# Softmax division moved behind the product with the values, the reciprocals broadcast through DRAM

## The chip, the cores and the metric

The kernel runs on one core of a Trainium2 chip. A core has five engines that run side by side, each with its own queue in program order: TensorE (PE, matrix products into PSUM), VectorE (DVE), ScalarE (ACT), GpSimd (POOL) and SyncE (SP, which here only issues DMAs). ACT and POOL issue DMAs too. The metric is the device time of one execution in microseconds (us); lower is better.

## The reference

Two layers of an encoder over 1024 tokens of width 1024. Layer 0 mixes tokens by windowed attention (16 query heads of 64, four key/value heads, a window of 128 to each side, a learned sink per head in the softmax); layer 1 by a gated linear recurrence (HGRN2). Each mixer also carries four cross-attention heads of 128 into 256 memory tokens. After each mixer comes a convolutional feed-forward part. What the change touches are the two softmaxes:

```python
# window attention (layer 0)
m = jnp.maximum(jnp.max(s, axis=-1, keepdims=True), sk)
p = jnp.exp(s - m)
p = p / (jnp.sum(p, axis=-1, keepdims=True) + jnp.exp(sk - m))
o = jnp.einsum('bnhgqk,bnkhd->bnqhgd', p.astype(v.dtype), vb)

# cross-attention into the memory (both layers)
p = jax.nn.softmax(s, axis=-1)
o = jnp.einsum('bhtm,bmhd->bthd', p.astype(v.dtype), v)
```

The sum belongs to a query and is the same for all values, so dividing the probabilities before the product or the result after it gives the same output up to rounding.

## The kernel before

All arithmetic is float32. Each operand of a matrix product is split into a high part (rounded to the matrix format, float32r) and a low part (the rest), and a product is two or three matmuls (`mm3`, lines 80 to 83). The split is a cast on ACT and a subtraction on DVE (`split`, lines 85 to 87), so nearly every product needs both of them first.

The program runs in stages: `start` (memory keys and values, transposed input), `window` (layer 0's mixer), the output projection `wo0`, `ffn` of layer 0, `hgrn` (layer 1's mixer), `wo1`, `ffn` of layer 1. The instructions are written down in program order, but the order on each engine is made by a planner that simulates a timeline with estimated costs (line 1559) and takes, among the instructions that are ready, those written earlier first; `tc.high_priority` and `tc.issue_after` bend this at single places. Within an engine's queue the resulting order is fixed: an instruction that waits holds up all behind it. Tiles come from pools with a number of buffers per tag; a tile whose buffers are all in use makes its writer wait until the oldest is free.

**Window attention** (`window`, lines 243 to 430). For each of the four key/value groups g, `proj(g)` computes queries, keys and values of its four heads, and `attend(g)` works in blocks of 128 queries, 32 blocks in all. A block, for its four heads j, makes the scores on PE (`ps`, two banks, L363 and L364), adds the mask and takes the maximum on DVE (L366), exponentiates on ACT with the sum as a by-product (L373), adds the sink and takes the reciprocal `rd`, 128 x 4, queries over partitions (L378, L379). It then multiplies the probabilities `sm` by `rd`: heads 0 and 1 on ACT (L382), 2 and 3 on DVE (L384). For each of two or three key tiles PE transposes the probabilities into `pt` (L389), they are split into `ph` and `pl`, and PE multiplies with the values into `po` (one bank, L392 and L393). The values stand in `v` as 64 columns of high part and 64 of low part, so that `po` holds on partitions 0 to 63 and 64 to 127 two halves of the output, transposed: value dimension over partitions, four heads times 128 queries along the free axis. ACT copies the upper half out (L395) and DVE adds the lower half (L396) into `o`, a tile of 64 partitions that takes a pair of blocks (two buffers). SP stores each pair to the DRAM tensor `oT` (L407), or for the last group into `ul` directly (L401), from where `split_moved` splits it.

**Cross-attention** (`cross_unit`, lines 198 to 240) handles one of four heads h and one half b of the tokens (512) in a unit. Eight units run inside `attend` of layer 0 (two each in the first two groups, four in the third), eight in layer 1's `hgrn`, in its heads 0 to 3. A unit projects its queries, makes scores for four query tiles, takes maximum, exponential, sum and reciprocal (L217 to L226), multiplies the probabilities `xp` by the reciprocals on DVE (L228, four instructions of 128 x 256), transposes (L233), splits, and multiplies with the values into `po`. ACT copies the result to `xo` (L239; one buffer; in layer 1 its tag is `ot`, shared with the recurrence's outputs, and the last unit uses the tile of the probabilities) and issues its store to `oT` itself (L240). In layer 0 the bank `po` is the one that the window blocks use; in layer 1 the two halves use different banks.

On SP's queue in these stages stand the weight loads (`wunit`, L75: DMA into the staging tile `st`, cast on ACT, subtraction on DVE or for some units on GpSimd, L77), the memory keys and values (L192), the stores of `o`, and the output projection's reads of `oT` (L456, L472). On GpSimd stand the additions of the rotary embedding (L288, L289) and DMAs that sum weights for the feed-forward part (L142, L144).

Of the kernel before, what the change touches and what calls it, by code (L numbers as in the profile page):

```python
# [8 lines left out]
F32 = mybir.dt.float32  # L9
# [3 lines left out]
AF = mybir.ActivationFunctionType  # L13
ALU = mybir.AluOpType
# [4 lines left out]
P = 128  # L19
# [28 lines left out]
def build(tc, A, out):  # L48
    nc = tc.nc
    act, dve, pool, pe = nc.scalar, nc.vector, nc.gpsimd, nc.tensor  # L50
    bc = lambda ap, shape: ap.to_broadcast(shape)

    dram = tc.alloc_tile_pool(name="dram", bufs=1, space=DRAM)
    oT = [dram.tile([12, P, T], F32, name=f"oT{l}") for l in range(2)]
# [95 lines left out]
        next(x)  # L150

    kvd = [dram.tile([4, P, 2, 256], F32, name=f"kvd{l}") for l in range(2)]

    def memory_kv(tp, psb, mh, ml, first, rsb, rsm, step):
        held = []
# [42 lines left out]
    def cross_unit(l, h, b, head, wp, tags, w0, pair, dead=False):  # L198

        wh, wl, kvh, kvl = head  # L200
        ps = tags["pj"][2].tile([P, 512], F32, tag=tags["pj"][0], bufs=tags["pj"][1], name="pj")
        for k in range(KT):
            c = slice(k * P, (k + 1) * P)
            m = slice(b * 512, (b + 1) * 512)
            mm3(ps, wh[:, c], wl[:, c], uh[:, k, m], ul[:, k, m], k == 0, k == KT - 1)
        xh, xl = pair("x", b)
        with tc.high_priority(AHEAD):
            split(xh, xl, ps)
        p = wp.tile([P, 4, 256], F32, tag="sm", bufs=tags["sm"], name="xp")
        st = {x: wp.tile([P, 4], F32, tag=x, name=x) for x in ("nm", "su", "rd")}  # L210
        for i in range(2):
            s = tags["ps"][2].tile([P, 2, 256], F32, tag=tags["ps"][0], bufs=tags["ps"][1], name="ps")
            for j in range(2):
                m = slice((2 * i + j) * P, (2 * i + j + 1) * P)
                mm3(s[:, j, :], xh[:, m], xl[:, m], kvh[:, 0, :], kvl[:, 0, :], True, True)
            e = slice(2 * i, 2 * i + 2)
            dve.reduce_max(st["nm"][:, e], s, axis=AX.X)  # L217
            if l == 0:
                dve.tensor_tensor(st["nm"][:, e], st["nm"][:, e], xsc[:, 1, 4 * b + 2 * i:4 * b + 2 * i + 2], op=ALU.mult)
            else:  # L220
                dve.tensor_scalar_mul(st["nm"][:, e], st["nm"][:, e], -XSCALE)
            for j in range(2):
                q = 2 * i + j
                act.activation(p[:, q, :], s[:, j, :], AF.Exp, bias=st["nm"][:, q:q + 1],
                               scale=xsc[:, 0, 4 * b + q:4 * b + q + 1] if l == 0 else XSCALE, accum_out=st["su"][:, q:q + 1])
        dve.reciprocal(st["rd"], st["su"])  # L226
        for q in range(4):
            dve.tensor_scalar_mul(p[:, q, :], p[:, q, :], st["rd"][:, q:q + 1])  # L228
        po = tags["po"][b]()
        for m in range(2):  # L230
            tp = tags["pt"][2].tile([P, 4, P], F32, tag=tags["pt"][0], bufs=tags["pt"][1], name="pt")
            for q in range(4):
                pe.transpose(tp[:, q, :], p[:, q, m * P:(m + 1) * P], ident)  # L233
            ph, pl = pair("p", m)
            split(ph, pl, tp.rearrange("p a b -> p (a b)"))
            hd = slice(m * P, (m + 1) * P)
            mm3(po, kvh[:, 1, hd], kvl[:, 1, hd], ph, pl, m == 0, m == 1)
        ot = p[:, :2, :].rearrange("p a b -> p (a b)") if dead else w0.tile([P, 512], F32, tag=tags.get("xo", "xo"), bufs=1, name="xo")
        act.copy(ot, po)  # L239
        act.dma_start(oT[l][8 + h, :, b * 512:(b + 1) * 512], ot)  # L240


    def window():
# [4 lines left out]
        wmask = ap_.tile([P, 384], F32, bufs=1, name="wmask")  # L248
        sk = ap_.tile([P, 16], F32, bufs=1, name="sk")
        sk8 = ap_.tile([P, 16], F32, bufs=1, name="sk8")  # L250
        ap_.tile([64, 4, 256], F32, tag="o", bufs=2, name="o")
        nc.sync.dma_start(wmask, A["wmask"])
        nc.sync.dma_start(sk, A["a_sink"].to_broadcast([P, 16]))
        c4 = lambda ap: ap.rearrange("p (h a c) -> p h a c", a=2, c=32)
# [80 lines left out]
        pairs, roped = {}, {}  # L335
# [9 lines left out]
        def attend(g, qkv, blocks=range(NT)):  # L345
            qs, kh, kl, v = qkv
            for b in range(2):
                for nn in range(4):
# [1 line left out]
                    if n not in blocks:  # L350
                        continue
                    if nn % 2 == 0:
                        pairs[0] = ap_.tile([64, 4, 256], F32, tag="o", bufs=2, name="o")
                    o = pairs[0]
                    lo, hi = max(n - 1, 0), min(n + 2, NT)
                    w = (hi - lo) * P
                    mo = (lo - (n - 1)) * P
# [19 lines left out]
                            split_moved()  # L377
                    dve.tensor_tensor(st["su"], st["su"], st["es"], op=ALU.add)  # L378
                    dve.reciprocal(st["rd"], st["su"])  # L379
                    for j in range(4):  # L380
                        if j < 2:
                            act.activation(sm[:, j, :w], sm[:, j, :w], AF.Copy, scale=st["rd"][:, j:j + 1])  # L382
                        else:
                            dve.tensor_scalar_mul(sm[:, j, :w], sm[:, j, :w], st["rd"][:, j:j + 1])  # L384
                    po = psp.tile([P, 4, P], F32, tag="po", bufs=1, name="po")
                    for c in range(hi - lo):
                        tp = psp.tile([P, 4, P], F32, tag="pt", bufs=2, name="pt")
# [4 lines left out]
                        pe.matmul(po, v[:, lo + c, :], ph, start=c == 0, stop=False)  # L392
                        pe.matmul(po, v[:, lo + c, :], pl, start=False, stop=c == hi - lo - 1)  # L393
                    ov = o[:, :, (nn % 2) * P:(nn % 2 + 1) * P]
                    act.copy(ov, po[64:])  # L395
                    dve.tensor_tensor(ov, po[:64], ov, op=ALU.add)  # L396
                    if nn % 2 == 1 and g == 3:
                        ts_ = slice((n - 1) * P, (n + 1) * P)
                        moved.append(ts_)
# [1163 lines left out]
```

## Time and profile before

| | |
|---|---|
| median of 3 runs | 2662.74 us (2661.32 to 2666.62) |
| profiled execution, first to last instruction | 2663.0 us |
| TensorE busy | 2605.1 us, 98% of the span |
| VectorE, ScalarE, GpSimd busy | 1820.8, 1377.3, 468.3 us |
| mean granted TensorE clock | 0.998 |
| mean DMA rate | 160 GB/s |

The profile is one execution with the time of every instruction. A group line gives source line, engine, operation, output and input tiles, the count, the busy time and the mean of one in ns, then the time that the engine sat idle just before these instructions and what ended it. A wait line tells which engine waited at which line for which other, with the total in us, the number of times and the longest. A timeline line begins with the start and the duration in us. The view by stretches gives for each stretch (us from the span's start) the busy time and the number of instructions of each engine. Matmuls overlap, so that the busy times of single ones add up to more than the time TensorE spends.

### The profile page before, as it was taken

Reading aid. Unit: us, or ns where it says so; the run is one execution under the profiler, and the core shown is the slowest. Engines: PE = TensorE matmul, PEld = TensorE weight load, DVE = VectorE, ACT = ScalarE, POOL = GpSimd, SP = SyncE. Lnnn points to the kernel's source line nnn. Section 1 sums busy time; section 2 is a strip of 40 time slices with the busy share of each in tenths; the row PEclk is TensorE's granted clock in tenths of the full one; section 3 lists DMA queues with packets and bytes.
Section 4 is the critical chain, followed back from the end, with each engine's and each line's share of the span. In section 5 each row is a group of like instructions: output and inputs, shape, how many; then the busy total and the mean of one; then the engine's idle time right before and its main releaser. Section 6 shows DMA issues by size and latency. Waiting matters only on the chain. (4 is left out here: it accounts for less than half of the span.)

```text
span 2663.0 us, 39112 instructions
## 1 busy us (share of the span) xinstructions
PE 2605.1 (98%) x14420; PEld 2186.3 (82%) x14420; DVE 1820.8 (68%) x3043; ACT 1377.3 (52%) x2503; POOL 468.3 (18%) x520
## 2 busy tenths in 40 slices
PE   8999999999999999999999999999999999999998
PEld 7888887788888887887888888888887788888887
DVE  6778886578655565478688686887757755656447
ACT  6467676545444444455455554555534444444453
POOL 0321010211111100031224131231311111110013
PEclk9999999999999999999999999999999999999999
DMA  9772222367787857574235351103437778785666
GB/s 354 248 169 58 74 89 82 104 188 196 197 203 192 209 153 250 190 246 160 85 110 147 83 127 55 52 25 101 139 103 198 191 194 209 197 204 167 220 194 233
DMA packets 195728, 425.93 MB, mean 160 GB/s; under 512 B 20048, under 2 KB 56272, under 8 KB 189904
## 3 DMA queue, kind: packets, MB, share of 16 engines
q1 hardware_dynamic: 161552, 324.06, 37.6%
q0 software_dynamic: 24544, 90.19, 16.3%
q10 hardware_dynamic: 9440, 9.19, 1.1%
q8 instruction: 113, 1.85, 0.3%
q14 instruction: 79, 0.65, 0.1%
HBM read 330.04 MB, written 116.39 MB: 168 GB/s over the span
## 5 line engine op out<-in xcount | busy, mean ns | idle before, releaser
L87 DVE TENSOR_TENSOR wl<-st,wh 128x1024 fp32r<-128x1024 f32 (+1 forms) x238 | 263.4, 1113 | 318.4 <-ACT wh L86 308.1
L86 ACT CAST wh<-st 128x1024 fp32r<-128x1024 f32 (+1 forms) x238 | 222.5, 937 | 289.7 <-PE X L575 187.8
L81 PE MATMUL pj<-uh,wh 128*128 128x512 f32 x512 | 202.9, 397 | 4.0 <-DVE q L1118 2.0
L575 PE MATMUL X<-wl,wh 128*128 128x512 f32 x528 | 205.4, 391 | 0.3 <-DVE wl L87 0.3
L575 PE MATMUL X<-wh,wl 128*128 128x512 f32 x528 | 205.0, 390 | 0.0
L575 PE MATMUL X<-wh 128*128 128x512 f32 x528 | 199.6, 391 | 2.6 <-ACT c L989 2.1
L82 PE MATMUL pj<-ul,wh 128*128 128x512 f32 x512 | 201.7, 394 | 0.1
L83 PE MATMUL pj<-uh,wl 128*128 128x512 f32 x512 | 201.8, 394 | 0.0
L81 PE MATMUL pj<-wh,uh 128*128 128x384 f32 (+1 forms) x512 | 190.3, 373 | 4.7 <-DVE gs L1104 2.5
L83 PE MATMUL pj<-wh,ul 128*128 128x384 f32 (+1 forms) x512 | 187.7, 367 | 0.0
L82 PE MATMUL pj<-wl,uh 128*128 128x384 f32 (+1 forms) x512 | 187.3, 366 | 0.1
L77 DVE TENSOR_TENSOR wl<-st,wh 128x1024 fp32r<-128x1024 f32 (+1 forms) x91 | 116.3, 1283 | 26.0 <-ACT wh L76 25.3
L575 PE MATMUL V<-uh,wh 128*128 128x512 f32 x336 | 130.7, 389 | 0.0
L575 PE MATMUL V<-ul,wh 128*128 128x512 f32 x336 | 130.7, 389 | 0.0
L575 PE MATMUL V<-uh,wl 128*128 128x512 f32 x336 | 130.7, 389 | 0.0
L76 ACT CAST wh<-st 128x1024 fp32r<-128x1024 f32 (+1 forms) x97 | 97.7, 1013 | 44.9 <-PE pj L82 25.2
L575 PEld LDWEIGHTS X<-wh 128*128 128x128 f32 x528 | 99.5, 188 | 24.1 <-ACT c L989 2.5
L575 PEld LDWEIGHTS X<-wl,wh 128*128 128x128 f32 x528 | 99.6, 189 | 21.3 <-DVE wl L87 0.7
L575 PEld LDWEIGHTS X<-wh,wl 128*128 128x128 f32 x528 | 99.5, 188 | 20.7
L81 PEld LDWEIGHTS pj<-uh,wh 128*128 128x128 f32 x512 | 96.3, 188 | 24.2 <-DVE q L1118 3.1
L83 PEld LDWEIGHTS pj<-uh,wl 128*128 128x128 f32 x512 | 96.2, 188 | 18.6
L82 PEld LDWEIGHTS pj<-ul,wh 128*128 128x128 f32 x512 | 96.3, 188 | 18.6 <-DVE ul L87 0.4
(413 smaller groups left out, 7167.9 us busy)
## 6 DMA issues: line engine op xcount, KB each, us to landing
st<-hid SPq DMA_DIRECT2D x154, 256.0 KB, 3.0
st<-in_ffw_dram SPq DMA_DIRECT2D x108, 256.0 KB, 3.4
w2s<-in_ffw_dram POOLq DMA_DIRECT2D x24, 1024.0 KB, 8.4
st<-in_ffw_dram SPq DMA_DIRECT2D x46, 512.0 KB, 4.3
hid<-tt SPq DMA_DIRECT2D x88, 256.0 KB, 4.7
st<-w2s SPq DMA_DIRECT2D x88, 256.0 KB, 3.4
sx<-in_ffw_dram SPq DMA_DIRECT2D x84, 256.0 KB, 4.0
sy<-in_ffw_dram SPq DMA_DIRECT2D x42, 512.0 KB, 6.6
```

What stands on the lines that cost most here:

```text
L76: act.copy(h[:, :n], raw)
L77: (eng or dve).tensor_tensor(l[:, :n], raw, h[:, :n].bitcast(F32), op=ALU.subtract)
L81: pe.matmul(o, ah, bh, start=first, stop=False)
L82: pe.matmul(o, ah, bl, start=False, stop=False)
L83: return pe.matmul(o, al, bh, start=False, stop=last)
L86: act.copy(h, src)
L87: dve.tensor_tensor(l, src, h.bitcast(F32), op=ALU.subtract)
L575: last = pe.matmul(o, x, y, start=new, stop=e, skip_group_check=not first)
```

## The change

A helper `spread(dst, rd)` writes the 128 x 4 reciprocals into one of 48 rows of a new DRAM tensor `rdd`, transposed so that the four heads (or query tiles) with their 128 queries lie one behind the other, and then reads that row back into `dst`, the same row for every partition. Both DMAs are issued by SP.

In the cross-attention the four multiplications of the probabilities go. The output tile first receives the spread reciprocals, and DVE multiplies `po` by them into the same tile, in place of ACT's copy. SP issues the store, no longer ACT. In layer 1's last unit, where the output tile is that of the probabilities, the spread comes after the last transpose.

In the window attention the four multiplications (L382, L384) go. The tile `o` has 128 partitions now; the lower 64 take the result as before, in the upper 64 one half of the columns takes the unnormalised sums of the two parts of `po` (ACT's copy and DVE's addition, as before but to these partitions) and the other half the spread reciprocals; which half is which alternates with the block. GpSimd multiplies the two into the lower 64 partitions.

```diff
+    rdd = dram.tile([48, 4, P], F32, name="rdd")
+    slots = iter(range(48))
+
+    def spread(dst, rd):
+
+        row = rdd[next(slots)]
+        nc.sync.dma_start(row.rearrange("j p -> p j"), rd)
+        nc.sync.dma_start(dst, row.unsqueeze(0).to_broadcast(list(dst.shape)))
...
         dve.reciprocal(st["rd"], st["su"])
-        for q in range(4):
-            dve.tensor_scalar_mul(p[:, q, :], p[:, q, :], st["rd"][:, q:q + 1])
+        if not dead:
+            ot = w0.tile([P, 512], F32, tag=tags.get("xo", "xo"), bufs=1, name="xo")
+            spread(ot.rearrange("p (q c) -> p q c", q=4), st["rd"])
         po = tags["po"][b]()
...
-        ot = p[:, :2, :].rearrange("p a b -> p (a b)") if dead else w0.tile([P, 512], F32, tag=tags.get("xo", "xo"), bufs=1, name="xo")
-        act.copy(ot, po)
-        act.dma_start(oT[l][8 + h, :, b * 512:(b + 1) * 512], ot)
+        if dead:
+            ot = p[:, :2, :].rearrange("p a b -> p (a b)")
+            spread(ot.rearrange("p (q c) -> p q c", q=4), st["rd"])
+        dve.tensor_tensor(ot, po, ot, op=ALU.mult)
+        nc.sync.dma_start(oT[l][8 + h, :, b * 512:(b + 1) * 512], ot)
...
-                        pairs[0] = ap_.tile([64, 4, 256], F32, tag="o", bufs=2, name="o")
-                    o = pairs[0]
+                        pairs[0] = ap_.tile([P, 4, 256], F32, tag="o", bufs=2, name="o")
+                    o = pairs[0][:64]
+                    sums, rows = [pairs[0][64:, :, x * P:(x + 1) * P] for x in (nn % 2, 1 - nn % 2)]
...
                     dve.reciprocal(st["rd"], st["su"])
-                    for j in range(4):
-                        if j < 2:
-                            act.activation(sm[:, j, :w], sm[:, j, :w], AF.Copy, scale=st["rd"][:, j:j + 1])
-                        else:
-                            dve.tensor_scalar_mul(sm[:, j, :w], sm[:, j, :w], st["rd"][:, j:j + 1])
+                    spread(rows, st["rd"])
                     po = psp.tile([P, 4, P], F32, tag="po", bufs=1, name="po")
...
-                    act.copy(ov, po[64:])
-                    dve.tensor_tensor(ov, po[:64], ov, op=ALU.add)
+                    act.copy(sums, po[:64])
+                    dve.tensor_tensor(sums, po[64:], sums, op=ALU.add)
+                    pool.tensor_tensor(ov, sums, rows, op=ALU.mult)
```

2 lines of the change are left out of this document (1 added, 1 removed).

## The prediction

> **What bounds the kernel now.** I read the page's first part, then the busy time by stretch, then who kept TensorE waiting.
>
> ```profile
> PE 2605.1 (98%) x14420; PEld 2186.3 (82%) x14420; DVE 1820.8 (68%) x3043; ACT 1377.3 (52%) x2503; POOL 468.3 (18%) x520
> ```
>
> ```profile
> core 0: us, PE busy (x) PEld busy (x) DVE busy (x) ACT busy (x) POOL busy (x), PEclk, DMA share, GB/s
> 100.00:200.00 100.00, 93.17 (x519) 83.09 (x520) 74.86 (x201) 63.28 (x165) 23.07 (x31) 0.97 0.73 173
> 200.00:300.00 100.00, 96.83 (x563) 86.91 (x562) 84.14 (x224) 70.07 (x177) 14.69 (x20) 1.00 0.29 71
> 300.00:400.00 100.00, 92.58 (x533) 81.00 (x533) 81.00 (x212) 72.61 (x180) 11.26 (x16) 1.00 0.26 78
> 400.00:500.00 100.00, 95.07 (x464) 76.68 (x463) 65.84 (x166) 64.43 (x150) 0.00 (x0) 1.00 0.23 68
> 1300.00:1900.00 600.00, 592.41 (x4737) 501.38 (x4736) 464.44 (x917) 316.98 (x688) 158.24 (x166) 1.00 0.32 88
> ```
>
> TensorE computes for 98% of the span, and the edit takes no matmul and no transpose away. So it can only win TensorE's idle time, in the two stretches where attention runs: 22.4 us in 100 to 500 (the window attention of layer 0 with its eight cross-attention units), 7.6 us in 1300 to 1900 (the eight units of layer 1). Their sum, 30 us or 1.1%, is the ceiling. Who ended those waits in 100 to 500 (engine and line, total us, times, longest):
>
> ```profile
> PE ps L363 <- DVE mx L366: 8.8, 14, 1.5
> PE po L393 <- DVE pl L87: 3.4, 6, 1.2
> PE pj L81 <- DVE xl L87: 1.5, 3, 0.9
> PE po L392 <- ACT ph L86: 1.2, 2, 0.8
> PE pt L389 <- ACT sm L382: 0.8, 2, 0.6
> ```
>
> None is over 1.5 us: TensorE waits for VectorE or ScalarE because those run behind, not for one long chain. Only the last row, 0.8 us, waits for the division itself.
>
> **The change part by part.** *Removed.* Groups of instructions in 95 to 505 (busy us, mean ns of one, then the idle time before):
>
> ```profile
> L382 ACT ACTIVATE sm<-sm,rd 128x384 f32<-128x384 f32 (+1 forms) x64 | 34.1, 584 | 5.9 <-DVE rd L379 5.8
> L384 DVE TENSOR_SCALAR sm<-sm,rd 128x384 f32<-128x384 f32 (+1 forms) x64 | 23.9, 416 | 0.5
> L228 DVE TENSOR_SCALAR xp<-xp,rd 128x256 f32<-128x256 f32 x32 | 14.6, 519 | 0.4
> L239 ACT COPY xo<-po 128x512 f32<-128x512 f32 x8 | 4.6, 581 | 5.9 <-PE po L83 5.9
> L396 DVE TENSOR_TENSOR o<-po,o 64x512 f32<-64x512 f32 x32 | 21.7, 677 | 6.0 <-ACT o L395 5.9
> ```
>
> ScalarE loses 34.1 + 4.6 = 38.7 us. VectorE loses 23.9 + 14.6 and gains eight products of 128 x 512 out of PSUM in place of the copy; the nearest row is L396, 0.68 us each, so 5.4: net 33.1. (The copy and add of the two halves, L395 and L396, stay; they only write to partitions 64 to 127.) Over these 400 us VectorE's load falls from 305.8 to 272.7 (76% to 68%), ScalarE's from 270.4 to 231.7 (68% to 58%).
>
> What TensorE gets of it I estimate by how a queue's backlog shrinks, taking it as busy over idle: VectorE 0.765/0.235 = 3.26 before, 0.682/0.318 = 2.14 after, a third less. The waits of the kind above that end on a busy VectorE or ScalarE (8.8 + 3.4 + 1.5 + 1.2 + some 2.1 in smaller rows) are 17.0 us: a third is 5.8, and the 0.8 of L382 goes whole. Bounds: 0, if the order in which the planner puts the instructions passes nothing on, and 17.8.
>
> *Added on GpSimd*: 32 products of 64 x 512, both inputs in SBUF. A row for 64 partitions is missing; the nearest is the 128 x 512 product:
>
> ```profile
> L539 POOL TENSOR_TENSOR v<-v,g x4: 1294/1295/1761, 1920.7 to 1936.3; 128x512 f32<-128x512 f32 x4
> ```
>
> (min/median/max ns.) 32 x 1.295 = 41.4 us, 10% of the 400, on an engine that is at most 23% busy there. GpSimd isn't free for VectorE, though. A timeline shows it, first GpSimd's line, then VectorE's:
>
> ```profile
> 92.18 3.62 POOL L77 TENSOR_TENSOR wl<-st,wh 128x768 fp32r<-128x768 f32 x2
> ```
>
> ```profile
> 91.89 3.94 DVE L369 TENSOR_SCALAR nm<-mx 128x4 f32<-128x4 f32 x1
> ```
>
> A VectorE instruction on 4 elements a partition, else 0.16 us, lasted 3.94 us and ended at 95.83, just behind the two GpSimd products (95.80). The Trainium skill ("SBUF — State Buffer", section on the two separate sides) calls this an exclusive lock: a GpSimd instruction shuts out VectorE instructions with two SBUF inputs or in a two-port mode for its whole length. By that rule all 41.4 us could fall on VectorE and the gain would be below nothing; the row agrees on the mechanism, and how many meet is the question. In my own count, the instructions of this kind in the 400 us are nm, es and su of each block (3 x 32) and about 40 subtractions from SBUF, 136 in all; each meets a GpSimd product with 10% chance and loses half of it, 0.65 us: 8.8 us (bounds 0 and 41.4). That leaves 33.1 - 8.8 = 24.3 us of relief, load 70.4%, backlog 2.38, and the gain falls from 5.8 to 17.0 x (1 - 2.38/3.26) = 4.6. With the 0.8: **5.4 us won**.
>
> *Added on SP*: 48 spreads, each a write of 128 x 4 reciprocals (4 bytes apiece) into DRAM, a wait for it, and a read that broadcasts 2 KB to 64 or 128 partitions; the 16 stores of L240 move from ScalarE's queue to SP's. No DMA here writes 4-byte pieces. Nearest by size and by form (KB, median us from issue to landing):
>
> ```profile
> bng<-in_b_norm_g_dram SPq DMA_DIRECT2D x1, 4.0 KB, 2.1
> sk<-in_a_sink_dram SPq DMA_DIRECT2D x1, 8.0 KB, 4.7
> oT<-o SPq DMA_DIRECT2D x24, 128.0 KB, 2.7
> oT<-xo ACTq DMA_DIRECT2D x15, 256.0 KB, 2.8
> L240 ACTq DMA_DIRECT2D oT<-xo x15: 326/326/336, 206.1 to 1837.0; - x15
> ```
>
> The write: between 2.1 (small load) and 4.7 (the one broadcast, in a crowded start); I take 3 for its 512 pieces. The read: 2.7 to 4.7; I take 2.8, as for 256 KB. With two issues of 0.33 (L240) a spread takes some 6.5 us (5.5 to 10.1). Its cover is the way from the reciprocal to the point where the product is taken out of PSUM. The tightest pair of all 32 blocks, and the ends of the last two:
>
> ```profile
> 405.80 0.18 DVE L379 RECIPROCAL rd<-su 128x4 f32<-128x4 f32 x1
> ...
> 413.29 0.68 DVE L396 TENSOR_TENSOR o<-po,o 64x512 f32<-64x512 f32 x1
> ```
>
> ```profile
> 496.95 0.68 DVE L396 TENSOR_TENSOR o<-po,o 64x512 f32<-64x512 f32 x1 [0.81 <-ACT o L395]
> ...
> 500.18 0.68 DVE L396 TENSOR_TENSOR o<-po,o 64x512 f32<-64x512 f32 x1 [0.72 <-ACT o L395]
> ```
>
> 7.3 us at the tightest: hidden, at nothing. Without cover it would be 6.5 us a unit. In the window the one who waits is GpSimd, behind whose product the rope additions and the second-weight DMAs stand; PSUM is released by ScalarE and VectorE as before. On SP, behind the spread's two waits, stand the output stores L407, the weight loads L75 and the reads of oT; their buffers are filled a whole group ahead, so I put that at nothing too.
>
> Two covers are thinner. First, an odd block's broadcast goes into the columns that the even block's sums occupy, so it waits for that block's GpSimd product. For the last pair: 496.95 + 0.6 + 1.3 = 498.9, +0.3 + 2.8 = 502.0, +1.3 = 503.3 where L396 now ends at 500.8: the last output slips 2.5 us. TensorE has the output projection to do then; nothing. Second, in a cross unit the broadcast goes into the output tile itself (one buffer), so the second half's waits until the first half's result is stored; and there VectorE waits, holding the only po bank. The four pairs:
>
> ```profile
> 205.47 0.59 ACT L239 COPY xo<-po 128x512 f32<-128x512 f32 x1 [0.85 <-PE po L83]
> ...
> 211.25 0.59 ACT L239 COPY xo<-po 128x512 f32<-128x512 f32 x1
> ```
>
> ```profile
> 296.32 0.57 ACT L239 COPY xo<-po 128x512 f32<-128x512 f32 x1
> 302.96 0.57 ACT L239 COPY xo<-po 128x512 f32<-128x512 f32 x1
> ```
>
> ```profile
> 338.90 0.59 ACT L239 COPY xo<-po 128x512 f32<-128x512 f32 x1 [0.45 <-PE po L83]
> 348.77 0.56 ACT L239 COPY xo<-po 128x512 f32<-128x512 f32 x1
> ```
>
> ```profile
> 393.77 0.59 ACT L239 COPY xo<-po 128x512 f32<-128x512 f32 x1
> 401.87 0.59 ACT L239 COPY xo<-po 128x512 f32<-128x512 f32 x1 [4.59 <-PE po L83]
> ```
>
> Product 0.68, store 0.33 + 2.8, broadcast 0.33 + 2.8: 6.9 us against gaps of 5.8, 6.6, 9.9 and 8.1. Late by 1.1 and 0.3; I charge **1.0** (0 to 1.4). Layer 1's last unit broadcasts into the probabilities' own tile, so only behind its last transpose: one spread of 48, at most its 6.5 us; TensorE has other heads' work there, nothing. Layer 1 has banks for both halves; there VectorE loses 8 x (4 x 0.35 - 0.68) = 5.8 us of 464.4, 1.2%, and even if all of the 7.6 us that TensorE idles there hung on VectorE, a twentieth of backlog would bring no more than 0.4; I take **0.2**.
>
> **Sum.** -5.4 + 1.0 - 0.2 = -4.6 us against the profiled span of 2663.0: 2658.4. Span and median of the runs (2662.74) agree within 0.3, so I say **2658**.
>
> **The rivals.**
> *A, the whole backlog goes.* The planner may pull the transposes up, since they now follow the exponential directly; the 17.8 us of waits would fall by three quarters: 2663 - 13 = 2650. For it: the rows are all short. Against: VectorE stays near 70%.
> *B, nothing arrives.* The relief is eaten by GpSimd's lock (beyond 33.1 of its 41.4 us) or by the planner's order: 2662, for the 0.8 of L382. For it: the 3.94 us row. Against: it would need most products to meet such an instruction.
> *C, slower: the single output tile.* With landings L the chain from first to second half is 1.34 + 2L; four chains less the gaps of 30.4 us in all is 8L - 25. It outweighs the 5.6 won from L = 3.8 us, and from 4.5 is seen as slower. At the 4.7 of the broadcast row: 12.6 late, 2662.7 - 5.6 + 12.6 = 2670. For it: that row is the only broadcast in the trace. Against: it stands in the crowded start, 2.8 is the rule later.
> *D, the 4-byte write is the bound.* SP works in order, and 40 spreads in 400 us leave 10 us each. At twice the broadcast row, 9.4 us, for the write a spread is 12.9: 40 x 2.9 = 116 us more, 2773 with the 5.6 won. It decides from 6.5 us. The Trainium skill ("DMA: Bandwidth & Descriptors", rules for kernel authors) speaks against the write: a non-contiguous last dimension costs a descriptor per element, and a transpose by a rearranged pattern 19 times one in hardware. By that rule D or worse would follow. No run here shows a DMA of that form. Against D by rows: 2 KB, and bng's 128 pieces of 32 bytes landed in 2.1.
>
> **How the numbers follow.** Forecast 0.37 (2654 to 2661), A 0.23, B 0.21, C 0.15, D 0.04. Less than 0.2% (5.3 us) can't be told from no change here, so faster means under 2657.4. Faster: 0.17 of the forecast and A, 0.40. Same: 0.20 of the forecast, 0.18 of B, 0.38. Slower: C, D, and 0.03 of B, 0.22. The range 2646 to 2671 goes from beyond A's middle to C's; D and half of C's upper part are left out. The likeliest's own range is 2654 to 2661.
>
> **What would show it.** Right: TensorE idles 15 to 19 us in 100 to 500 instead of 22.4; VectorE there at some 70%; the waits ps<-mx near 6 us; no TensorE row that ends on a DMA. The spread: write and broadcast landing in 3 and 2.8 us. The lock: nm, es or su of over 1 us beside the new GpSimd products, some 9 us in all. C: po waits behind xo. D: SP's loads late, ScalarE waiting for st. Wrong if idle time grows outside these stretches, because the planner reordered work that I took as fixed.

## The result, and the profile after

The changed kernel takes 2826.8 us (median; 2817.66 to 2827.44) against 2662.74, a ratio of 1.0604 with an interval of 1.059 to 1.0618. I had said 2658. The profiled execution has a span of 2820.5 us, 157.5 more than before. First the busy time of the whole span, then by stretch (us of the stretch, busy time and instructions of each engine, granted TensorE clock, DMA share, GB/s):

```profile
PE 2641.6 (94%) x14420; PEld 2212.9 (78%) x14420; DVE 1794.0 (64%) x2931; ACT 1342.8 (48%) x2423; POOL 510.0 (18%) x552
```

```profile
100.00:200.00 100.00, 66.27 (x337) 59.60 (x336) 46.43 (x133) 40.07 (x109) 15.87 (x20) 0.81 0.64 119
200.00:300.00 100.00, 70.64 (x366) 61.29 (x364) 45.97 (x121) 38.43 (x96) 23.57 (x25) 0.85 0.66 105
300.00:400.00 100.00, 75.44 (x403) 64.81 (x403) 57.46 (x137) 44.43 (x111) 20.68 (x22) 0.91 0.31 58
400.00:500.00 100.00, 80.20 (x427) 70.69 (x427) 53.06 (x142) 44.45 (x120) 12.14 (x15) 0.89 0.39 51
500.00:600.00 100.00, 69.56 (x314) 56.44 (x313) 50.02 (x122) 45.92 (x109) 9.97 (x10) 0.85 0.28 78
1300.00:1900.00 600.00, 591.71 (x4365) 496.64 (x4364) 472.19 (x875) 315.82 (x652) 168.31 (x173) 1.00 0.41 117
```

Layer 0's attention, which ended near 500 us, now runs to about 660. TensorE's idle time in the span, span less busy, went from 57.9 to 178.9 us: 121.0 of the 157.5. The other 36.5 are in its busy time: the same 14420 matmuls last longer (the largest group of the attention, L81's products of 128 x 384, 374 ns each in place of 347), and the granted clock, 0.97 to 1.00 here before, is 0.81 to 0.91 where TensorE idles for a fifth to a third of the time. The Trainium skill ("TensorE: Matmul & The Clock Gate", Part 1) says that the gate follows how busy TensorE has recently been; the trace agrees. Layer 1, with its eight spreads, is as before: in 1300 to 1900 TensorE is busy for 591.71 us (592.41 before), and in 1460 to 2060, where the same work now stands, for 591.6.

Why is TensorE idle? The spread's two DMAs on SP's queue, in time (start, duration of the issue; L159 is the write of the reciprocals, L160 the broadcast that waits for it):

```profile
118.53 0.55 SPq L159 DMA_DIRECT2D rdd<-rd  x1
128.26 0.58 SPq L160 DMA_DIRECT2D o<-rdd  x1
128.94 0.80 SPq L75 DMA_DIRECT2D st<-in_wqkv_dram  x1
129.83 0.63 SPq L159 DMA_DIRECT2D rdd<-rd  x1
145.08 0.58 SPq L160 DMA_DIRECT2D o<-rdd  x1
145.71 1.35 SPq L416 DMA_DIRECT2D oT<-o  x2
147.15 0.54 SPq L159 DMA_DIRECT2D rdd<-rd  x1
166.77 0.59 SPq L160 DMA_DIRECT2D o<-rdd  x1
```

From a write to its broadcast pass 9.7, 15.3 and 19.6 us. All 48 writes, from issue to landing, and SP's wait for them (total, times, longest):

```profile
DMA to landing us min/median/max: 8.5/11.2/19.8
```

```profile
SPq L160 <- DMA rdd<-rd: 312.9, 30, 19.0
```

The write that I took at 3 us takes 11.2. Who waits in 100 to 660 us, in the view of waits:

```profile
POOL o L405 <- DMA o<-rdd: 225.2, 16, 27.7
PE ptq L322 <- POOL rq L299: 40.7, 7, 15.7
DVE rd L234 <- DMA rdd<-rd: 35.3, 5, 13.7
DVE xo L250 <- DMA xo<-rdd: 35.2, 4, 17.3
DVE rd L391 <- DMA rdd<-rd: 20.4, 6, 10.3
PE po L400 <- DVE o L404: 16.0, 5, 12.4
...
ACT uh L467 <- DMA ul<-oT: 36.2, 3, 17.1
ACT kvh L202 <- DMA kvl<-kvd: 31.0, 3, 16.7
ACT oh L86 <- DMA ol<-oT: 22.0, 4, 10.9
```

No row says that TensorE waits for a DMA. GpSimd waits 225.2 us for broadcasts in front of its product; behind the product stand its rotary additions, and TensorE waits 40.7 us for those, a third of its new idle time; its other waits end on VectorE and ScalarE. VectorE waits for the writes before it may reuse the reciprocals' two buffers (`rd`), and for the broadcast in the cross units. ScalarE waits for three kinds of load on SP's queue (L467 and L86 for the output projection's reads of `oT`, L202 for the memory keys and values): 89.2 us, where the same three took 12.0 before. And transfers that have nothing to do with the spread are late. KB each and median us to landing, first after in 100 to 700 us, then before in 100 to 600:

```profile
st<-in_wqkv_dram SPq DMA_DIRECT2D x7, 384.0 KB, 14.2
w2s<-in_ffw_dram POOLq DMA_DIRECT2D x4, 1024.0 KB, 16.8
```

```profile
w2s<-in_ffw_dram POOLq DMA_DIRECT2D x5, 1024.0 KB, 10.3
st<-in_wqkv_dram SPq DMA_DIRECT2D x8, 384.0 KB, 4.9
```

The DMA engines are busy longer for what they move: in 200 to 300 us 0.66 of the time at 105 GB/s, before 0.29 at 71 GB/s.

### The profile page after: what moved, and what is told of

It is laid out like the page before. It is cut to its first block, busy times and chain, and to the rows that moved or that the text cites. A ratio compares the mean times of both kernels' runs of the same rounds, so it can differ in the third digit from the quotient of the medians.

```text
span 2820.5 us, 39211 instructions
## 1 busy us (share of the span) xinstructions
PE 2641.6 (94%) x14420; PEld 2212.9 (78%) x14420; DVE 1794.0 (64%) x2931; ACT 1342.8 (48%) x2423; POOL 510.0 (18%) x552
## 5 line engine op out<-in xcount | busy, mean ns | idle before, releaser
L86 ACT CAST wh<-st 128x1024 fp32r<-128x1024 f32 (+1 forms) x238 | 222.5, 937 | 289.4 <-PE X L584 192.2
L81 PE MATMUL pj<-wh,uh 128*128 128x384 f32 (+1 forms) x512 | 195.5, 384 | 19.8 <-DVE v L310 16.2
L81 PE MATMUL pj<-uh,wh 128*128 128x512 f32 x512 | 203.4, 398 | 2.2 <-DVE xl L87 1.3
L77 DVE TENSOR_TENSOR wl<-st,wh 128x1024 fp32r<-128x1024 f32 (+1 forms) x91 | 116.3, 1286 | 31.0 <-ACT wh L76 30.9
L81 PEld LDWEIGHTS pj<-wh,uh 128*128 128x128 f32 x512 | 100.8, 197 | 32.5 <-issue 10.1
L86 ACT CAST ph<-pt 128x512 fp32r<-128x512 f32 x120 | 68.8, 585 | 99.6 <-PE pt L397 41.5
L967 POOL TENSOR_TENSOR c<-c,g 128x512 f32<-128x512 f32 x24 | 42.5, 1786 | 390.4 <-PE X L584 161.1
```

The costliest lines, as they stand in the source:

```text
L77: (eng or dve).tensor_tensor(l[:, :n], raw, h[:, :n].bitcast(F32), op=ALU.subtract)
L81: pe.matmul(o, ah, bh, start=first, stop=False)
L86: act.copy(h, src)
L967: pool.tensor_tensor(y[q][:, t, :], y[q][:, t, :], g3[:, c], op=ALU.mult)
```

## The experiments

Ratios are against the kernel before, with their intervals. The edits are shown in part.

### Which half: cross units or window blocks

Only the cross units changed, with the window blocks wholly as before (no GpSimd products either); then only the window blocks.

```diff
 # against the kernel after, shortened
 # cross units only: the window divides sm before the transposes
-                    spread(rows, st["rd"])
-                    pool.tensor_tensor(ov, sums, rows, op=ALU.mult)
+                    for j in range(4): (ACT or DVE multiplies sm[:, j] by rd)
 # window only: the cross units divide p before the transposes
-            spread(ot.rearrange("p (q c) -> p q c", q=4), st["rd"])
+        for q in range(4): dve.tensor_scalar_mul(p[:, q, :], ...)
```

> Only the cross-attention part of the change; the window attention divides as before. 16 spreads are left, 8 of them in layer 0. Theory S (SyncE stands still while each 4-byte write lands, 11.2 us in the changed kernel's trace, so that spreads in layer 0 run one after the other): 8 of 40 spreads, at most a fifth of the 164 us lost, and a unit has 18 us of cover or more, so 2662 to 2695 us. Rival G (the GpSimd products and their lock on VectorE make the loss): none of them is left, so no change, 2657 to 2663.

> Only the window part of the change; the cross-attention divides as before. Theory S: 32 of 40 spreads remain, 2760 to 2810 us, and no wait of VectorE for a cross unit's broadcast. Rival G: all 32 GpSimd products remain, so the whole loss does, 2815 to 2830.

Measured: 2698.0 us (1.0134, 1.0115 to 1.0154) and 2764.6 us (1.0392, 1.0373 to 1.0411). By these ratios sixteen spreads cost some 36 us, 32 cost 104 and both together 161, some 20 more than the sum. Both halves have the fault, and they make each other worse. The cross units alone fall just outside the 2662 to 2695 of theory S; rival G is out, since without any GpSimd product 36 us are still lost.

### The write's pieces

One line of the kernel after is changed: each partition writes its four reciprocals as one piece of 16 bytes, 128 in place of 512 of 4.

```diff
-        nc.sync.dma_start(row.rearrange("j p -> p j"), rd)
+        nc.sync.dma_start(row.rearrange("j p -> (j p)").rearrange("(p j) -> p j", j=4), rd)
```

> The changed kernel with the write of the reciprocals as 128 pieces of 16 bytes in place of 512 of 4; the rest, the wait and the broadcast, is the same. The reciprocals arrive in another order, so the division is by wrong numbers. Theory S: the time is in the 4-byte pieces; the write lands in 2 to 4 us and the kernel takes 2655 to 2685 us. Rival W (any write to DRAM followed by a read of it is too slow, whatever its pieces): the write still lands in 8 us or more and the time stays above 2780. Rival G: unchanged, 2815 to 2830.

Measured: 2661.7 us (1.0003, 0.9993 to 1.0012). By line and tiles, TensorE's matmuls stand in the order of the kernel after but for 2 of 14420, so it is not the planner's order that costs the 164 us. The landing of its writes:

```profile
DMA to landing us min/median/max: 1.4/2.4/15.1
```

The loss of 164 us against the kernel before hangs on those 4-byte pieces, in this one line.

### What such a write costs by itself

Transfers on an idle core: writes of several shapes one after another, and a load of 512 KB beside them, from three queues.

> Not the kernel: only DMAs, one after another, on an otherwise idle core, all the computation left out. The write of 128 x 4 reciprocals as 512, 256 and 128 pieces of 4 bytes, as 128 of 16 and 4 of 512; then a 512 KB load issued beside a write, from SyncE's, ScalarE's and GpSimd's queue. If a 4-byte piece has a price (theory T), the write takes some 9, 5.5 and 3.5 us for 512, 256 and 128 pieces and 2 for the others, and a load beside the 4-byte write lands 6 to 9 us later than beside none; if only on SyncE's queue, the pieces hold up their own queue, if on all three, the DMA engines. If the write is slow only in the crowd of the full kernel (rival C), it lands in under 4 us here in all forms.

Each write is followed by a read of its row, which is issued when the write has landed. Alone, 512 pieces of 4 bytes took 7.8 to 9.4 us until then, 256 took 7.6 to 7.75, 128 took 6.4 to 7.15; 128 pieces of 16 bytes 1.4 and 4 of 512 bytes 1.2. The time falls much less than the number of pieces. Beside the load (L96; L64 is the 4-byte write, L74 a broadcast, L97 the copy that waits for the load, in brackets its wait):

```profile
145.25 0.34 SPq L96 DMA_DIRECT2D lo<-in_xT_dram  x1
145.69 0.59 SPq L74 DMA_DIRECT2D b<-row  x1
149.01 0.69 DVE L97 COPY big<-lo 128x1024 f32<-128x1024 f32 x1 [3.79 <-DMA lo<-in_xT_dram]
149.43 0.38 SPq L64 DMA_DIRECT2D row<-rd  x1
...
149.93 0.43 SPq L96 DMA_DIRECT2D lo<-in_xT_dram  x1
158.53 0.58 SPq L74 DMA_DIRECT2D b<-row  x1
162.85 0.69 DVE L97 COPY big<-lo 128x1024 f32<-128x1024 f32 x1 [12.95 <-DMA lo<-in_xT_dram]
```

The load takes 12.9 us here (from issue to copy) instead of 3.8; loads without such a write took 3.8 to 5.2 in this probe. Issued from ScalarE's and GpSimd's queues beside such a write it keeps the copy waiting 11.46 and 11.72 us, so more than SP's queue is held. The Trainium skill ("DMA: Bandwidth & Descriptors", "Issuing engines are not separate DMA queues") says that all queues share the same 16 DMA engines; these three numbers agree.

Is it any piece of 4 bytes, or 4-byte pieces side by side? A second probe gives each form a line of its own:

```diff
+        s(d4, rd[:, 0:1])           # L69: 128 x 4 B, 4 B apart
+        s(d16[:, 0:1], rd[:, 0:1])  # L71: 16 B apart (L73: 32, L75: 64, L77: 512)
+        s(d8, rd[:, 0:2])           # L79: 128 x 8 B, side by side
+        s(row.rearrange("j p -> p j"), rd)            # L83: 512 x 4 B, as in the kernel
+        s(q64[:, :, 0].rearrange("j p -> p j"), rd)   # L85: 512 x 4 B, 64 B apart
```

> Only transfers on an otherwise idle core, one after another on SP's queue, each form on a line of its own: 128 pieces of 4 B written to DRAM at a stride of 4, 16, 32, 64 and 512 B, 128 pieces of 8 B and of 16 B next to each other, 512 pieces of 4 B next to each other and 64 B apart, and 16-byte pieces within SBUF. The kernel computes nothing of the reference. Theory H (small writes into the same stretch of DRAM are done one after another): the 4-byte pieces at 64 and 512 B land in 1.4 to 2.5 us like 16-byte pieces, those at 4 B in 6.4 to 7.2 us as in the probe before, and the strides of 16 and 32 B in between. Theory N (any 4-byte write to DRAM is slow): all strides land in 6 to 9 us. The 512 pieces 64 B apart tell the same: under 4 us by H, 7.8 to 9 us by N.

Each line is followed by its read-back on SP, which starts when the write has landed (start, issue):

```profile
59.05 0.34 SPq L69 DMA_DIRECT2D d<-rd  x1
66.26 0.34 SPq L70 DMA_DIRECT2D rd<-d  x1
69.47 0.32 SPq L71 DMA_DIRECT2D d<-rd  x1
70.86 0.32 SPq L72 DMA_DIRECT2D rd<-d  x1
...
82.23 0.32 SPq L79 DMA_DIRECT2D d<-rd  x1
84.97 0.32 SPq L80 DMA_DIRECT2D rd<-d  x1
...
91.09 0.37 SPq L83 DMA_DIRECT2D row<-rd  x1
99.16 0.37 SPq L84 DMA_DIRECT2D rd<-row  x1
102.81 0.36 SPq L85 DMA_DIRECT2D q<-rd  x1
104.63 0.36 SPq L86 DMA_DIRECT2D rd<-q  x1
```

The probe makes four rounds, and these lines are of one. Over the four, 128 pieces of 4 bytes took 7.2 to 9.2 us side by side and 1.4 at 32, 64 and 512 bytes apart; 16 bytes apart they took 1.4 to 5.7 (median 2.3). Pieces of 8 bytes side by side took 2.6 to 2.9, of 16 bytes 1.4 to 1.8. The kernel's form took 8.1 to 10.3, and the same 512 pieces 64 bytes apart 1.8 to 2.0. So neither the size nor the number of the pieces alone makes it slow, but how many of them fall on the same few bytes of DRAM. That such neighbours are written one after another, each with a read of what surrounds it, would fit; no run shows the inside of it. The Trainium skill ("DMA: Bandwidth & Descriptors", "Specifications") puts at 512 bytes the limit below which a DMA engine reads, modifies and writes. By that alone 16-byte pieces would suffer too; at 1.4 us they don't, so here the neighbours decide and not the size.

### Held transfers or waiting engines

In the first of these the broadcast reads a row written once at the start, so nobody waits for the small writes to be read; in the second the reciprocals also have 8 buffers in layer 0; in the third there is no broadcast at all and nobody reads the writes; in the fourth there are no spreads.

```diff
 # ready row (the second has bufs 8 for rd as well)
-        nc.sync.dma_start(dst, row.unsqueeze(0).to_broadcast(list(dst.shape)))
+        nc.sync.dma_start(dst, ready.unsqueeze(0).to_broadcast(list(dst.shape)))
 # writes alone: no broadcast, bufs 8, identity in place of the rows; without spreads: no write either
+                    pool.tensor_tensor(ov, sums, bc(ident[64:].unsqueeze(1), [64, 4, P]), op=ALU.mult)
```

> The changed kernel, but each broadcast reads one row that was written at the start (of -0.5), so nothing waits for the 4-byte writes; these are still issued, and land as late as they did. The division is left out of the result. Theory S: SyncE no longer stands still, 2655 to 2680 us. Rival T (the 4-byte pieces clog the DMA engines for all other transfers): stays above 2720, and the broadcasts still land in 4.5 us or more. Rival G: 2815 to 2830.

> The kernel whose broadcasts read a row written at the start (2769.5), with eight buffers in layer 0 for the reciprocals in place of two, so that VectorE's next reciprocal waits for no 4-byte write either (it did, 53 us in all). The division is left out of the result. If the rest of that loss was this wait (theory B), 2655 to 2675. If it is the 4-byte writes holding up all other transfers (theory T, as beside the lone write: a load of 4.5 us took 12 to 13 from any of the three queues), 2700 to 2765, with weight loads still landing in 10 us or more.

> The kernel after, with the division left out and no broadcast: the 48 writes of 4-byte pieces are issued and nobody reads them or waits for them, with 8 buffers of reciprocals in layer 0; GpSimd and VectorE multiply by the identity instead. The output is the product with the values, not divided. Theory T (the small writes hold the transfer engines and so delay every other load and store): well over the 2649 us of the kernel without the spreads, 2700 to 2760 us. Theory W (it is the waiting for the broadcast and the order that the planner makes of it that costs): 2648 to 2665 us.

> The changed kernel without its 96 spread DMAs: GpSimd and VectorE multiply by the identity matrix in SBUF in place of the reciprocals, same shapes. The division is left out of the result. The 16-byte run took 2661.7 us, so that without any of the loss the change won nothing. Theory L (what the removed divisions won is given back by the lock of GpSimd's products on VectorE): 2659 to 2663, while the run with no division at all is at 2655 or below. Rival R (the spreads' waits on SyncE and GpSimd gave it back): 2653 to 2657.

| kernel | us | ratio, interval | TensorE busy and idle in its span |
|---|---|---|---|
| after | 2826.8 | 1.0604 (1.059 to 1.0618) | 2641.6, 178.9 |
| ready row | 2769.5 | 1.0409 (1.0389 to 1.043) | 2634.5, 134.9 |
| ready row, 8 buffers | 2758.4 | 1.036 (1.0346 to 1.0375) | 2633.7, 126.0 |
| writes alone | 2722.2 | 1.0223 (1.0209 to 1.0237) | 2620.4, 100.2 |
| no spreads | 2649.2 | 0.9952 (0.994 to 0.9964) | 2599.9, 47.5 |

Read from below, each added to the ones before it: 48 writes that nobody reads cost 73 us. The broadcasts, late behind such writes, add 36. Waiting for `rd` to be free again adds 11, and waiting for the write itself 57. The kernel with no spreads came out below both of its ranges. In the kernel with the writes alone, in 100 to 600 us (KB each and median us to landing, then who waits there):

```profile
w2s<-in_ffw_dram POOLq DMA_DIRECT2D x5, 1024.0 KB, 18.7
...
w2s<-in_ffw_dram POOLq DMA_DIRECT2D x4, 768.0 KB, 17.5
...
PE po L398 <- DVE o L402: 33.5, 5, 21.1
ACT o L401 <- DMA oT<-o: 27.8, 1, 27.8
```

The first two are GpSimd's queue, on which no spread stands; without spreads these loads landed in 10.2 and 8.0 us. I had named SP's queue as the thing that a slow write would hold; it holds transfers of the other queues too. But SP's queue has its part even where nobody waits for a write: the issue of two stores of `o` behind the writes lasted 23.2 us there (146.6 to 169.8), ScalarE waited 27.8 us for that tile to be free, and TensorE's longest stall, 21.1 us, stands behind it. So the 73 us are not the work of GpSimd's late loads alone, and how they divide is open.

### What the removed division is worth

The kernel before without its multiplications, and one in which GpSimd makes ScalarE's share of them.

```diff
 # no division: the four multiplications of the window and of the cross units left out
 # GpSimd:
-                            act.activation(sm[:, j, :w], sm[:, j, :w], AF.Copy, scale=st["rd"][:, j:j + 1])
+                            pool.tensor_scalar_mul(sm[:, j, :w], sm[:, j, :w], st["rd"][:, j:j + 1])
```

> The kernel before with the multiplications by the reciprocals simply left out (not divided at all): the most that moving them can win. By the backlog estimate of the prediction, 5.8 + 0.8 us: 2654 to 2656. Theory N (TensorE's short waits don't shrink with ScalarE's and VectorE's load, the planner's order sets them): 2659 to 2663.

> The kernel before with one edit: in the window attention GpSimd instead of ScalarE divides the probabilities of heads 0 and 1; no DMA is added. The run without any division won 12.5 us, and the one with GpSimd's products but no spread won as much, so GpSimd's lock costs nothing measurable. Theory U (ScalarE's and VectorE's relief is what wins, whoever takes the work): ScalarE's part, 34 of the 72 us taken away in all, goes: 2653 to 2659. Rival L2 (GpSimd's instruction is longer than ScalarE's 0.6 us and now stands between exponential and transpose): 2661 or more.

Measured: 2649.5 us (0.9951, 0.9937 to 0.9965) without the division; 2665.95 (1.0012, 1.0003 to 1.0021) with GpSimd. Two readings follow. The kernel after without its spreads (2649.2) and the kernel before without its division (2649.5) are equal, so the 32 GpSimd products and any lock on VectorE cost nothing that can be measured in the time. And without the division some 13 us are won, below both ranges of that run. That is not the removed work alone: the planner makes another order for it, in which some 1100 of TensorE's 14420 matmuls stand elsewhere (by their tiles), and no run has the one without the other. With GpSimd dividing nothing is won, as rival L2 said: its product of 128 x 384 takes 1.39 us, ScalarE's took 0.58. The busy rows, with no spreads and with no division:

```profile
PE 2599.9 (98%) x14420; PEld 2184.0 (82%) x14420; DVE 1791.2 (68%) x2931; ACT 1341.2 (51%) x2423; POOL 506.2 (19%) x552
```

```profile
PE 2602.5 (98%) x14420; PEld 2187.8 (83%) x14420; DVE 1779.8 (67%) x2915; ACT 1350.3 (51%) x2439; POOL 467.3 (18%) x520
```

Of TensorE's idle time, 57.9 us before, 47.5 and 45.9 are left; its busy time is 5.2 and 2.6 us shorter as well.

To see whose share of the division counts, three kernels let TensorE divide: the turn of the probabilities multiplies by the identity times the reciprocals, and the multiplications shrink from up to 128x384 to 128x128. First for ScalarE's two heads, then VectorE's; both turn the other two heads by a plain matmul as well. The third has VectorE's heads alone so.

```diff
 # the third
+                    dg = ap_.tile([P, 2, P], F32, tag="dg", bufs=1, name="dg")
-                            dve.tensor_scalar_mul(sm[:, j, :w], sm[:, j, :w], st["rd"][:, j:j + 1])
+                            dve.tensor_scalar_mul(dg[:, j - 2, :], ident, st["rd"][:, j:j + 1])
-                            pe.transpose(tp[:, j, :], sm[:, j, c * P:(c + 1) * P], ident)
+                            pe.matmul(tp[:, j, :], sm[:, j, c * P:(c + 1) * P], dg[:, j - 2, :], start=True, stop=True)
```

> The kernel before, but the heads 0 and 1 of each window unit are divided by TensorE: ScalarE writes the identity times the reciprocals (128x128 for each head) and the turn of the probabilities multiplies by it instead of by the identity. No DMA is added and no wait for one; ScalarE's 64 multiplications shrink from 128x384 to 128x128, VectorE's and the cross units stay. Theory D2 (the 12.5 us of the removed work are had in proportion as ScalarE's and VectorE's time before the turn shrinks, if no transfer takes its place): some 13 to 16 us less of ScalarE, 0 to 5 us won, 2657 to 2663 us. Rival P (a product with a matrix that is not the identity, as a plain matmul, costs TensorE more than the turn of 273 ns): with 176 of them, 2667 us and more.

> The same for the heads 2 and 3, whose division VectorE makes: its 64 multiplications shrink from 128x384 (438 ns) to 128x128, ScalarE's stay. Theory D2: 12 to 15 us less of VectorE, 0 to 6 us won, 2656 to 2663 us, and more than with ScalarE's if VectorE is the one that TensorE waits for. Rival P: 2667 us and more.

> The run before on VectorE's heads turned the heads 0 and 1 by a plain matmul as well, and each plain matmul of a 128x128 tile stands in the trace as two instructions of 275 ns where the turn is one of 273 ns: 352 instructions more than before, 176 of them for nothing. Here the heads 0 and 1 are turned as before and only the heads 2 and 3 by the matmul with the identity times the reciprocals. With c for 176 more instructions and g for the smaller work of VectorE, the run before gave 2c - g = +11.2 us, this one gives c - g. Theory D2 with g of some 6 to 10 us: c is 9 to 11 us, and this is within 3 us of before, 2662 to 2667 us. Rival (VectorE's share of the division is worth nothing, g = 0): c is 5.6 us and this is 2670 us.

Measured: 2683.7 us (1.0077, 1.0063 to 1.009), 2675.8 (1.0053, 1.004 to 1.0066) and 2661.7 (0.9999, 0.999 to 1.0008). The first two are rival P's. A plain float32 matmul is two instructions of 275 ns where the turn is one. The third kernel's rows in 95 to 505:

```profile
L393 PE MATMUL pt<-dg,sm 128*128 128x128 f32 x352 | 54.4, 275 | 0.0
...
L391 PE MATMUL pt<-ident,sm 128*128 128x128 f32 x176 | 35.1, 273 | 0.5 <-ACT sm L383 0.4
```

```profile
PE 2616.4 (98%) x14596; PEld 2206.1 (83%) x14596; DVE 1810.3 (68%) x3043; ACT 1380.5 (52%) x2503; POOL 473.9 (18%) x520
```

By times alone my two equations, 2c - g = 11.2 and c - g = 0.2, would give 11 us for VectorE's share. The busy rows don't allow that: TensorE's idle time is 40.9 us here, 41.0 and 41.9 in the other two. It is the same whichever engine is relieved and however many instructions TensorE got. Added TensorE work may cover waits by itself, so these runs can't say whose share counts. Open.

### Keeping the gain

Four forms without 4-byte neighbours. TensorE turns the reciprocals to 4 rows of 512 bytes before the write (layer 0 only). The row keeps the 16-byte order and the product reads it with a stride. The same, with the first group dividing as before. And the strided form, but with GpSimd's window products reading the identity, so that nobody waits for those broadcasts.

```diff
 # turned by TensorE, copied by DVE
+        pe.transpose(tp, rd, ident)
+        nc.sync.dma_start(row, rt)
 # 16-byte rows
+                    pool.tensor_tensor(v4(ov), v4(sums), rows.rearrange("c s (u j) -> c j s u", j=4), op=ALU.mult)
 # late: spread for g > 0, as before for g == 0; unread: ident[64:] in place of rows
```

> The changed kernel with the reciprocals turned by TensorE (128 x 4 to 4 x 128, one transpose of 0.14 us a spread, a copy out by VectorE), so that the write is 4 rows of 512 bytes; in layer 0 only (layer 1 divides as before). Theory S/T (the 4-byte pieces alone make the loss): the write lands in 2 to 3.5 us and the kernel takes 2658 to 2672 us, some 6 us of it for 40 transposes. Rival W (the way through DRAM costs in itself): above 2690.

> The changed kernel with the write as 128 pieces of 16 bytes, made right: the row keeps the order query by head, is broadcast in that order, and the product reads it with a stride. Same DMAs as in the run with 16-byte pieces that took 2661.7: 2655 to 2664. If the product's stride of 16 bytes costs VectorE or GpSimd (rival V), above 2666.

> As the run before this in the list, but the eight blocks of the first group divide as the kernel before does; 24 blocks and the cross units keep the moved division. In the 16-byte run the spreads of the first 100 us land in up to 15 us, beside the copies of the feed-forward weights (DMA share 0.82 there), and GpSimd's wait for one of them stops TensorE for 8.0 us. Theory F (the spread's wait in that crowd gave the 12.5 us back): 2649 to 2656. Rival Y (every spread gives some of it back, by SyncE's and GpSimd's waits all along): 2657 to 2662.

> The version with 16-byte pieces, but GpSimd multiplies the window units by the identity, so nobody waits for their broadcast; its transfers are issued as before, and the cross units divide as in that version. The window units are left undivided. If the 12.5 us that the 16-byte version gives back go to GpSimd's wait for the broadcast: 2649 to 2655 us. If they go to the transfers themselves, to SP's waiting for them or to the order that the planner makes of them: 2660 to 2666 us, as the version that reads them.

| | us | ratio, interval |
|---|---|---|
| turned by TensorE | 2664.2 | 1.0008 (1.0 to 1.0017) |
| 16-byte rows | 2663.55 | 1.0003 (0.9994 to 1.0012) |
| 16-byte rows, first group as before | 2664.57 | 1.0008 (0.9999 to 1.0017) |
| 16-byte rows, unread in the window | 2660.07 | 0.9985 (0.9976 to 0.9994) |

None that divides beats the kernel before. The last one, undivided in the window, fell on the lower end of its second range, 2660 to 2666. It is 3.5 us faster than the one that reads the rows, but that is not the price of GpSimd's wait: GpSimd's products are shorter too (1.33 us, with the stride 1.57), and the largest stall only takes another road. TensorE's largest wait in 100 to 500, with 16-byte rows and then with them unread:

```profile
PE ptq L324 <- POOL rq L301: 7.7, 1, 7.7
...
PE ptq L324 <- DVE qs L335: 8.0, 2, 7.8
```

In the first GpSimd had stood 15.7 us before a broadcast of the first group, in the second VectorE had stood 9.5 us before a write of that group, to use `rd` again. Of TensorE's idle time in 100 to 500, 25.4 and 23.9 us against 15.4 without spreads, this one stall is most of the difference. Dividing the first group as before takes the stall away (no single wait of TensorE there is over 2.5 us), yet the time, 2664.57, is above both of its ranges. The planner's order is not a likely cause of the loss in the first run with 16-byte pieces (2661.7): its matmuls stand as in the kernel with no spreads (2649.2) but for some 140 of 14420. TensorE's idle time with 16-byte rows is 56.8 us, as before (57.9), with stalls at other places. What exactly takes the remainder is open.

## Why the prediction was wrong

*The write* is the step that failed: "The write: between 2.1 (small load) and 4.7 (the one broadcast, in a crowded start); I take 3 for its 512 pieces." It landed in 8.5 to 19.8 us, median 11.2, above my upper bound from the first to the last. Both rows that I bounded it by are loads into SBUF, and one of them is the 128 pieces of 32 bytes that I set against rival D. In the second probe reading the 4-byte pieces back took 2.2 to 3.4 us, within my bounds; writing them took 7.2 to 9.2. The trace held no DMA that writes neighbours of a few bytes, and I let rows of the other direction close the range.

*Its cover* fell with it: 7.3 us at the tightest was enough for a spread of 6.5. With 11.2 for the write and 4.5 for the broadcast (median; 2.8 forecast) a spread is 16.4 with its issues. GpSimd's wait of 225.2 us came where the prediction placed it, in front of the product, and went on to TensorE through the rotary additions (40.7 us).

*"their buffers are filled a whole group ahead, so I put that at nothing too"* failed as well, for the reads of `oT` that it names: ScalarE waited 58.2 us for them (36.2 and 22.0), 10.2 before. For the staged weights it held: no wait of ScalarE for them shows up, though they landed in 14.2 us instead of 4.9. And it looked at SP's queue only. The missing terms are that such a write delays the transfers of all queues (73 us with nobody waiting for the write itself, a part of it on SP's queue) and that the two buffers of `rd` are held until it lands (11 us).

*Rival D*, to which I gave 0.04, comes nearest: its bound, the write, is what happened. Its working, with the measured write, gives 11.2 + 3.5 less the 10 us between spreads, 40 times 4.7, or 2845 with the 5.6 won; 2826.8 was measured. That nearness is luck: D lays everything on SP's wait for the write, which by the ready row is 57 us of the loss, and with the measured broadcast of 4.5 the same sum gives over 2900. By its rule from the Trainium skill ("DMA: Bandwidth & Descriptors", rules for kernel authors) a non-contiguous last dimension costs a descriptor per element, and the result agrees in direction. The second probe narrows the rule: 512 elements 64 bytes apart land in 1.8 us.

*The gain* came, and larger. I had 5.4 us from the backlog and 0.2 in layer 1; without any spreads it is 13. In 100 to 500 TensorE's idle time falls from 22.4 to 14.1 us without the division, 8.3 where I had 5.4, and the waits ps<-mx, 8.8 us before and forecast near 6, are at 1.9 there and at 4.3 in the kernel with no spreads. It stays under the ceiling of 30. Whether the backlog or the planner's new order brought it isn't shown, and rival A, which laid 13 us on the planner, had the size. The rest I can't place by stretch, since the later stages shift.

*GpSimd's products* were right in size: 1.32 us each in the kernel after, 1.29 forecast. The 8.8 us that I charged VectorE for the lock, which brought the gain from 5.8 to 4.6, are not there: the window's nm, es and su, the instructions that I let the products lock out, take 20.4 us in all before, 20.5 in the kernel with no spreads and 20.4 in the kernel after. The one long nm of 3.94 us, beside L77, stands in all three.

*Rival C*, the single output tile, can't be told apart in the kernel after, since its waits (35.2 us at `xo`) hang on the same writes. With 16-byte pieces VectorE still waits for the broadcast at `xo`, 8.4 us in two waits; whether that reaches TensorE isn't shown. *B*, nothing arrives, is what a spread without the fault gives (1.0003), though not by its reasons: the gain is there (rival A's size) once the spreads are gone, and with them it is taken back.

## What to carry to other kernels

A DMA's price depends on its direction and on how its pieces lie at the destination: bound an unknown write by a row that writes, and if there is none, leave the upper end open and give the rival its weight. A DMA that writes neighbouring elements of 4 bytes into DRAM delayed the transfers of every queue here, so look for its cost in loads of other queues; give each piece 16 bytes or spread the pieces out. No TensorE row need name the DMA that stops it: follow the engine that TensorE waits for, and what stands ahead on that engine's queue.

## What the runs showed of the hardware

- A write of 128 pieces of 4 bytes side by side in DRAM landed in 7.2 to 9.2 us on an idle core, 32 or more bytes apart in 1.4; 512 in the kernel's form in 8.1 to 10.3, 64 bytes apart in 1.8 to 2.0.
- Beside such a write a 512 KB load took 11 to 13 us on any of the three queues, without it 3.8 to 5.2.
- The granted TensorE clock fell to 0.81 to 0.91 where TensorE was 66 to 80% busy, and TensorE's busy time grew by 36.5 us beside 121 us more of idle time.
- 32 GpSimd products of 64 x 512 (42 us) lengthened the window's VectorE instructions on 4 elements by nothing (20.4 us before, 20.4 and 20.5 with them).
- A plain float32 matmul of 128x128 by 128x128 is two instructions of 275 ns, the transpose one of 273.
